# A transformer of two blocks on one core: squares of the norms between stages split over two engines, and next weights released at another point

## The chip, the cores and the metric

The kernel runs on 1 core of one Trainium2 chip, as one launch. The metric is the time of an execution in device microseconds (us); several executions are timed and their median is given. A profile is one further execution, recorded by the hardware profiler.

## The reference

x holds 256 tokens of 1024 fp32 channels. The first block has two layers of `proj = rms_norm(x) @ w_in`, attention beside a long convolution, and `x = x + rms_norm(m @ w_out)`. The second block has four stages, each of this form, with shift, scale and gate from a condition vector:

```python
h = rmsnorm(x, norm) * (1.0 + sc) + sh
y = stage(h)      # even_mixer, dense swiglu, s5_mixer, moe_swiglu
x = x + g * y
```

The norm is `x * rsqrt(mean(x * x) + eps)`: over the 1024 channels of each token the squares are summed, and every stage's first product needs it.

## The kernel before

**Tiles.** Tokens lie on the partitions, in two token tiles of 128 (`tt` 0 and 1), x is 128x1024 for each. Products are made in three parts: an fp32 operand is split (`split`, lines 205 to 211) into a high part, rounded by ScalarE (ACT, line 208), and a low part, the rest, by VectorE (DVE, line 211); `mm3` (lines 219 to 223) then adds high by high, low by high and high by low on TensorE (PE). Names end accordingly: `whi`, `wlo` for a chunk of weights (128x1024, made by `wchunk` from `raw`, which a DMA of SP's queue fills), `hTh`, `hTl` for the normed input with channels on the partitions.

**Between stages.** When the last stage has added its output to token tile `tt`, it calls `x_done(tt)`. This squares x and sums (`row_stats`: two halves of 512 channels, both on ACT, line 368), makes 1/sqrt on DVE in some eight instructions of 128x1 (`norm_stats`, lines 330 to 360), writes that factor on a diagonal `dg` (DVE, line 421), and `transposed` lets PE multiply x by it, 8 products of 128x128 in two groups of four (line 440; the trace shows two rows for each), which turns and scales x at once. DVE, or ACT for the first group, applies gain and shift (`hh`, lines 447 to 454) and `split` makes hTh and hTl of it. The places where this happens are called here: start (layer 0, 0 to 25 us), A (layer 0 to layer 1, at 285), B (to the mixer, at 560), C (to the dense FFN, at 722), D (to S5, at 932, kind "chunk") and E (to the experts, at 1060, kind "both", where z is made in place of dg and the router's product comes first); the others are of kind "plain". So 6 places by 2 tiles by 2 halves give 24 squares.

**Order.** The program is written stage by stage; a list scheduler then lays down for every engine one queue, which the engine runs in order. `issue_after(i)` keeps an instruction behind instruction i in it. In "plain" places the splits of the next two chunks of weights (HOLDP is 2) are held behind `self.hold`, the last ACT instruction so far, which there is the second square of tile 1; "chunk" holds none (HOLDC is 0), "both" holds four behind another point. PRIO, HH_BUFS (3 buffers for `hh`) and the rest of the numbers stay.

Of the kernel before, what the change touches and what calls it, by code (L numbers as in the profile page):

```python
# [14 lines left out]
AF = mybir.ActivationFunctionType  # L15
ALU = mybir.AluOpType
# [4 lines left out]
P = 128  # L21
# [97 lines left out]
class Net:  # L119
    def __init__(self, ctx, tc, a, out):  # L120
        self.ctx, self.tc, self.nc, self.a, self.out = ctx, tc, tc.nc, a, out
        self.uid, self.ring, self.extra, self.left, self.hold, self.held = 0, {}, 0, 0, None, 0
        self.tasks = []
        self.mq = tc.nc.gpsimd
        self.dq = (tc.nc.gpsimd, tc.nc.sync, tc.nc.scalar)[DQ]
        self.gate, self.pool_lo = [], 0
        self.rows, self.cols = {}, {}
        e = ctx.enter_context
        self.cst = e(tc.tile_pool(name="cst", bufs=1))
        self.act = e(tc.tile_pool(name="act", bufs=1))  # L130
        self.mod = e(tc.tile_pool(name="mod", bufs=1))
        self.sm = e(tc.tile_pool(name="sm", bufs=8))
        self.ps = e(tc.tile_pool(name="ps", bufs=1, space=PSUM))
        self.dram = e(tc.tile_pool(name="dr", bufs=1, space=DRAM))
        self.wp = e(tc.tile_pool(name="wp", bufs=1, reuse_waits="tile"))
        self.raws, self.hls = [(self.wp, RAW_BUFS)], [(self.wp, HL_BUFS)]
# [121 lines left out]
    def wchunk(self, src, k, n):  # L258

        out = []  # L260
        step = 1024 // n
        for k0 in range(0, k, step):
            kk = min(step, k - k0)
            raw = self.raw()[:, :kk * n]
            self.nc.sync.dma_start(raw.rearrange("p (k n) -> p k n", k=kk),
                                   src[k0 * P:(k0 + kk) * P].rearrange("(k p) n -> p k n", p=P))
            hi = self.turn(self.hls, "whi", F32R)[:, :kk * n]
            lo = self.turn(self.hls, "wlo", F32R)[:, :kk * n]
            self.pool_lo -= 1
            with self.tc.issue_after(self.hold) if self.held > 0 else nullcontext():  # L270
                self.split(hi, lo, raw, lo_eng="pool" if self.pool_lo >= 0 else "dve")
            self.held -= 1
            out += [(hi[:, i * n:(i + 1) * n], lo[:, i * n:(i + 1) * n]) for i in range(kk)]
        return out

# [86 lines left out]

    def row_stats(self, src):

        ss = []
        for n in range(2):
            ss.append(self.small())
            self.nc.scalar.activation(self.junk, src[:, n * 512:(n + 1) * 512], AF.Square, scale=1.0 / 32, accum_out=ss[n])
        return self.norm_stats(ss, 1e-6)

    def product(self, f, n=1):
# [24 lines left out]
    def x_done(self, tt):  # L396

        kind = self.nx[2]
        if self.hT is None:
            if kind == "both":  # L400
                self.hT = (self.t(self.act, [P, 8, S], "hTh"), None)
            else:
                self.hT = (self.t(self.act, [P, 8, S], "hTh", F32R), self.t(self.act, [P, 8, S], "hTl", F32R))
        x = self.x[:, tt, :]
        if kind == "both":
            rr = self.row_stats(x)
            after = self.latest(mybir.EngineType.Activation)
            self.z = [*(self.z if tt else ()), self.rows_z(tt, rr)]
            if tt == 1:
                with self.tc.issue_after(after) if T0_LAST else nullcontext():  # L410
                    self.transposed(0, self.z[0], None)
                self.transposed(1, self.z[1], None)
                self.hold, self.held = self.latest(mybir.EngineType.Activation), HOLD
                self.split_rows()
        else:

            rr = self.row_stats(x)
            if tt:
                self.hold, self.held = self.latest(mybir.EngineType.Activation), HOLDP if kind == "plain" else HOLDC
            dg = self.t(self.act, [P, P], "dg", bufs=2)  # L420
            self.nc.vector.tensor_scalar(dg, self.ident, *rr, ALU.mult, ALU.mult)
            self.transposed(tt, x, dg)
        self.set_gate("x")
        if tt == 1:
            self.pool_lo = POOL_LO
# [1519 lines left out]
HH_BUFS = 3  # L1945
# [126 lines left out]
HOLDP = 2  # L2072
HOLDC = 0
# [1 lines left out]
```

## Time and profile before

| | us |
|---|---|
| median of 3 runs | 1892.56 |
| range of the 3 runs | 1890.31 to 1893.56 |
| the profiled execution | 1882.28 |
| its span, first to last instruction | 1880.4 |
| PE busy | 1803.7 |
| DVE busy | 1517.6 |
| ACT busy | 1210.3 |

The profiled execution is one of its own and lies 10.3 us under the median; durations and waits are read from it. A busy time is the sum over an engine's instructions; the share of it over the whole span says little of a place where another engine sets the pace, so the places are read one by one. The mean granted clock of PE was 0.970 of full speed.

### The profile page before, as it was taken

How to read it: one execution, taken by the hardware profiler on the slowest of the kernel's cores; microseconds unless marked ns; L12 is line 12 of the kernel's file. 1: busy time of each engine (PE TensorE's matmuls, PEld its weight loads, DVE VectorE, ACT ScalarE, POOL GpSimd, SP SyncE). 2: the span in 40 equal slices, each digit the busy share in tenths (PEclk: the TensorE clock that was granted, in tenths of full speed). 3: DMA queues.
4: the chain of work that ended last, by engine and by line, in shares of the span. 5: the costliest groups of instructions: out<-in, count | busy, mean ns of one | idle time of the engine just before them, and what ended most of it. 6: DMA issues, size and time to landing. Idle time of an engine off the chain costs nothing.

```text
span 1880.4 us, 31046 instructions
## 1 busy us (share of the span) xinstructions
PE 1803.7 (96%) x11358; PEld 1536.1 (82%) x11358; DVE 1517.6 (81%) x2393; ACT 1210.3 (64%) x1670; POOL 195.9 (10%) x355
## 2 busy tenths in 40 slices
PE   7999998999999998999899899999999999999996
PEld 6887776988878768999799788888888888888875
DVE  6787667687558668975578789999999999999897
ACT  5664355564448526655454588887778787877775
POOL 0003232231330000111100100100001000100000
PEclk9999998999998969999998899999999999999998
DMA  7656785875775504988675779999999999999991
GB/s 258 202 155 214 247 287 199 282 250 199 255 248 166 167 12 144 291 258 256 218 264 215 272 266 378 340 355 343 377 344 349 348 380 355 346 373 356 344 355 44
DMA packets 268968, 503.45 MB, mean 268 GB/s; under 512 B 24690, under 2 KB 110516, under 8 KB 267272
## 3 DMA queue, kind: packets, MB, share of 16 engines
q1 hardware_dynamic: 247768, 445.84, 68.9%
q0 software_dynamic: 21040, 55.55, 8.4%
q8 instruction: 91, 1.49, 0.3%
q14 instruction: 69, 0.57, 0.1%
HBM read 485.35 MB, written 15.75 MB: 266 GB/s over the span
## 4 chain that ended last, share of the span: by engine, by line
PE 79%; issue 10%; DVE 5%; DMA 3%; ACT 2%; POOL 1%; POOLq 0%; ACTq 0%; DVEq 0%
PE A L221 12%; PE A L222 12%; PE A L223 12%; PE B L221 6%; PE B L222 6%; PE B L223 6%; PE A L323 4%; PE A L324 4%; PE A L325 4%; PE B L959 2%; DMA rawm<-in_e_mod_mix_w_dram 2%; DVE wlo L211 1%; PE B L440 1%; PE B L1756 1%; PE B L1101 1%
## 5 line engine op out<-in xcount | busy, mean ns | idle before, releaser
L211 DVE TENSOR_TENSOR wlo<-raw,whi 128x1024 fp32r<-128x1024 f32 x777 | 930.3, 1221 | 204.6 <-ACT whi L208 193.1
L208 ACT ACTIVATE whi<-raw 128x1024 fp32r<-128x1024 f32 x777 | 814.3, 1058 | 339.0 <-PE A L223 135.9
L221 PE MATMUL A<-whi,hTh 128*128 128x512 f32 (+1 forms) x752 | 285.6, 387 | 7.3 <-ACT hTh L208 4.8
L222 PE MATMUL A<-wlo,hTh 128*128 128x512 f32 (+1 forms) x752 | 289.2, 385 | 1.4 <-DVE wlo L211 1.2
L223 PE MATMUL A<-whi,hTl 128*128 128x512 f32 (+1 forms) x752 | 286.8, 383 | 0.9 <-DVE hTl L211 0.7
L323 PE MATMUL A<-hTh,whi 128*128 128x256 f32 x864 | 244.9, 284 | 3.8 <-ACT hTh L208 2.2
L324 PE MATMUL A<-hTl,whi 128*128 128x256 f32 x864 | 243.2, 282 | 0.8 <-DVE hTl L211 0.8
L325 PE MATMUL A<-hTh,wlo 128*128 128x256 f32 x864 | 243.7, 282 | 0.1
L221 PEld LDWEIGHTS A<-whi,hTh 128*128 128x128 f32 x752 | 142.3, 189 | 38.5 <-ACT hTh L208 5.9
L323 PEld LDWEIGHTS A<-hTh,whi 128*128 128x128 f32 x864 | 163.7, 190 | 7.9 <-issue 3.6
L222 PEld LDWEIGHTS A<-wlo,hTh 128*128 128x128 f32 x752 | 142.4, 189 | 33.8 <-DVE wlo L211 5.1
L223 PEld LDWEIGHTS A<-whi,hTl 128*128 128x128 f32 x752 | 142.3, 189 | 30.9 <-DVE hTl L211 2.1
L324 PEld LDWEIGHTS A<-hTl,whi 128*128 128x128 f32 x864 | 163.8, 190 | 2.7 <-DVE hTl L211 1.0
L325 PEld LDWEIGHTS A<-hTh,wlo 128*128 128x128 f32 x864 | 163.7, 190 | 2.0 <-issue 1.2
L222 PE MATMUL A<-wlo,xg 128*128 128x512 f32 (+1 forms) x384 | 143.2, 373 | 0.0
L223 PE MATMUL A<-whi,xg 128*128 128x512 f32 (+1 forms) x384 | 142.9, 372 | 0.0
L221 PE MATMUL A<-whi,xg 128*128 128x512 f32 (+1 forms) x384 | 141.6, 376 | 0.0
L222 PE MATMUL B<-wlo,mhh 128*128 128x512 f32 x352 | 138.6, 394 | 0.0
L223 PE MATMUL B<-whi,mhl 128*128 128x512 f32 x352 | 137.5, 391 | 0.0
L221 PE MATMUL B<-whi,mhh 128*128 128x512 f32 x352 | 120.8, 393 | 0.2 <-ACT mhh L208 0.2
L222 PEld LDWEIGHTS A<-wlo,xg 128*128 128x128 f32 x384 | 72.4, 189 | 12.9 <-DVE wlo L211 0.3
L223 PEld LDWEIGHTS A<-whi,xg 128*128 128x128 f32 x384 | 72.3, 188 | 12.5
(586 smaller groups left out, 2816.7 us busy)
## 6 DMA issues: line engine op xcount, KB each, us to landing
raw<-in_o_exp_up_dram SPq DMA_DIRECT2D x176, 512.0 KB, 5.7
raw<-in_o_exp_down_dram SPq DMA_DIRECT2D x176, 512.0 KB, 5.9
raw<-in_o_exp_gate_dram SPq DMA_DIRECT2D x174, 512.0 KB, 5.8
raw<-in_w_in_dram SPq DMA_DIRECT2D x96, 512.0 KB, 4.7
rawm<-in_e_mod_mix_w_dram POOLq DMA_DIRECT2D x24, 512.0 KB, 6.0
rawm<-in_e_mod_ffn_w_dram POOLq DMA_DIRECT2D x24, 512.0 KB, 6.1
rawm<-in_o_mod_mix_w_dram POOLq DMA_DIRECT2D x24, 512.0 KB, 5.6
rawm<-in_o_mod_ffn_w_dram POOLq DMA_DIRECT2D x24, 512.0 KB, 6.4
```

What stands on the lines that cost most here:

```text
L208: nc.scalar.activation(hi, src, AF.Copy)
L211: (nc.gpsimd if lo_eng == "pool" else nc.vector).tensor_tensor(lo, src, hi.bitcast(F32), ALU.subtract)
L221: nc.tensor.matmul(out, ah, bh, start=first, stop=False)
L222: nc.tensor.matmul(out, ah, bl, start=False, stop=False)
L223: nc.tensor.matmul(out, al, bh, start=False, stop=last)
L323: nc.tensor.matmul(o, wh[:, ms], xh[:, k, :], start=k == 0 and m == 0, stop=False, **kw)
L324: nc.tensor.matmul(o, wh[:, ms], xl[:, k, :], start=False, stop=False, **kw)
L325: nc.tensor.matmul(o, wl[:, ms], xh[:, k, :], start=False, stop=k == 7, **kw)
L440: nc.tensor.matmul(o, x[:, ks], dg, start=True, stop=True)
L959: nc.tensor.matmul(acc[32 * j:32 * j + 32, cs], silu[:, k:k + 1].broadcast_to([P, 32]), raws[i][:, k * P:(k + 1) * P], start=r == 0 and i ...
L1101: nc.tensor.matmul(pt[:, i, :], z[ps, ts], w[ps, ts], start=True, stop=True)
L1756: nc.tensor.transpose(ptr[:, i * P:(i + 1) * P], sg[:, i * P:(i + 1) * P], self.ident)
```

## The change

Of each norm's two squares the second is made on DVE, as one instruction that multiplies and sums (the trace shows it as a custom instruction and a read-out of 0.08 us; its product goes into a buffer of the ring `hh` and is not used). In `x_done` of kinds "plain" and "chunk" the hold is no longer the last square of tile 1 but `behind0`, the last ACT instruction of `transposed(0)`, which makes tile 0's hTh; and the first chunk after it (`spared`) isn't held. The `__init__` sets `spared` to 0.

```diff
@@ -267,9 +267,12 @@
             hi = self.turn(self.hls, "whi", F32R)[:, :kk * n]
             lo = self.turn(self.hls, "wlo", F32R)[:, :kk * n]
             self.pool_lo -= 1
-            with self.tc.issue_after(self.hold) if self.held > 0 else nullcontext():
+            with self.tc.issue_after(self.hold) if self.held > 0 and self.spared <= 0 else nullcontext():
                 self.split(hi, lo, raw, lo_eng="pool" if self.pool_lo >= 0 else "dve")
-            self.held -= 1
+            if self.spared > 0:
+                self.spared -= 1
+            else:
+                self.held -= 1
             out += [(hi[:, i * n:(i + 1) * n], lo[:, i * n:(i + 1) * n]) for i in range(kk)]
         return out
 
@@ -362,10 +365,10 @@
 
     def row_stats(self, src):
 
-        ss = []
-        for n in range(2):
-            ss.append(self.small())
-            self.nc.scalar.activation(self.junk, src[:, n * 512:(n + 1) * 512], AF.Square, scale=1.0 / 32, accum_out=ss[n])
+        ss = [self.small(), self.small()]
+        self.nc.scalar.activation(self.junk, src[:, :512], AF.Square, scale=1.0 / 32, accum_out=ss[0])
+        h = src[:, 512:]
+        self.nc.vector.tensor_tensor_reduce(self.t(self.act, [P, 4, P], "hh", bufs=HH_BUFS).rearrange("p k t -> p (k t)"), h, h, 1.0 / 1024, 0.0, ALU.mult, ALU.add, ss[1])
         return self.norm_stats(ss, 1e-6)
 
     def product(self, f, n=1):
@@ -416,10 +419,11 @@
 
             rr = self.row_stats(x)
             if tt:
-                self.hold, self.held = self.latest(mybir.EngineType.Activation), HOLDP if kind == "plain" else HOLDC
+                self.hold, self.held, self.spared = self.behind0, HOLDP if kind == "plain" else HOLDC, 1
             dg = self.t(self.act, [P, P], "dg", bufs=2)
             self.nc.vector.tensor_scalar(dg, self.ident, *rr, ALU.mult, ALU.mult)
             self.transposed(tt, x, dg)
+            self.behind0 = self.latest(mybir.EngineType.Activation)
         self.set_gate("x")
         if tt == 1:
             self.pool_lo = POOL_LO
```

Line numbers grow by 3 or 4 behind this (360 becomes 363, 421 becomes 424, 440 becomes 444, 447 becomes 451, 454 becomes 458); 208, 211 and 221 to 223 stay. Over the whole program DVE has 3039 rows in place of 3013, ACT 2151 in place of 2163 (12 squares and, in layer 0, 2 activation table loads fewer; some rows are grouped otherwise), PE 12408 for 12405 and SP 1422 for 1423 by grouping alone, POOL 224 as before.

DVE at the start. `sm` are the 128x1 values of a norm, `subln` is no part of it; `x_75` is x. Before, from the end of tile 0's norm to the first low part:

```order
L350 TENSOR_SCALAR sm_15_104<-sm_15_104 128x1
L421 TENSOR_SCALAR dg_110<-ident_78,sm_14_103,sm_15_104 128x128
L360 SCALAR_TENSOR_TENSOR sm_23_134<-sm_21_130,sm_22_132 128x1
L333 TENSOR_SCALAR sm_24_136<-sm_23_134 128x1
L342 SCALAR_TENSOR_TENSOR sm_25_138<-sm_24_136,sm_23_134 128x1
L347 SCALAR_TENSOR_TENSOR sm_26_139<-sm_25_138 128x1
L348 SCALAR_TENSOR_TENSOR sm_27_140<-sm_25_138 128x1
L349 SCALAR_TENSOR_TENSOR sm_26_139<-sm_26_139,sm_24_136 128x1
L350 TENSOR_SCALAR sm_27_140<-sm_27_140 128x1
L421 TENSOR_SCALAR dg_146<-ident_78,sm_26_139,sm_27_140 128x128
L447 TENSOR_TENSOR hh_117<-B_112,pre_83 128x512
L211 TENSOR_TENSOR wlo_172<-raw_169,whi_171 128x1024
```

Now, from tile 0's hh on (L371 is the square, its second row the read-out):

```order
L451 TENSOR_TENSOR hh_118<-B_113,pre_83 128x512
L211 TENSOR_TENSOR wlo_174<-raw_171,whi_173 128x1024
L451 TENSOR_TENSOR hh_127<-B_122,pre_83 128x512
L371 ISA hh_134,sm_23_132<-x_75 128x512
L371 ISA sm_23_132 128x1
L211 TENSOR_TENSOR hTl_93<-hh_118,hTh_92 128x4x128
L363 SCALAR_TENSOR_TENSOR sm_25_136<-sm_22_131,sm_23_132 128x1
L211 TENSOR_TENSOR hTl_93<-hh_127,hTh_92 128x4x128
L336 TENSOR_SCALAR sm_26_138<-sm_25_136 128x1
L211 TENSOR_TENSOR wlo_180<-raw_177,whi_179 128x1024
L345 SCALAR_TENSOR_TENSOR sm_27_140<-sm_26_138,sm_25_136 128x1
L211 TENSOR_TENSOR wlo_186<-raw_183,whi_185 128x1024
```

Tile 1's norm stood ahead of every low part, its dg (`dg_146`) ahead of tile 0's hh. It now stands behind the first, with two more inside; its dg follows five rows further down.

PE at the start, `A` being the products of tile 0 (A_167, now A_169) and tile 1 (A_168, now A_170). Before:

```order
L440 MATMUL B_112<-dg_110,x_75 128x128 x4
L440 MATMUL B_121<-dg_110,x_75 128x128 x4
L440 MATMUL B_148<-dg_146,x_75 128x128 x4
L440 MATMUL B_157<-dg_146,x_75 128x128 x4
L221 MATMUL A_167<-whi_171,hTh_92 128x512
L222 MATMUL A_167<-wlo_172,hTh_92 128x512
L223 MATMUL A_167<-whi_171,hTl_93 128x512
```

Now, the end of tile 0's 18 products and what follows:

```order
L221 MATMUL A_169<-whi_185,hTh_92 128x512
L222 MATMUL A_169<-wlo_186,hTh_92 128x512
L223 MATMUL A_169<-whi_185,hTl_93 128x512
L444 MATMUL B_150<-dg_148,x_75 128x128 x4
L444 MATMUL B_159<-dg_148,x_75 128x128 x4
L552 MATMUL B_255<-ffeat_247,fw_52_249 64x256
L221 MATMUL A_170<-whi_173,hTh_92 128x512
L222 MATMUL A_170<-wlo_174,hTh_92 128x512
L223 MATMUL A_170<-whi_173,hTl_93 128x512
```

Tile 1's eight transposes have moved from behind tile 0's to behind all 18 products of tile 0 with the first three chunks. At A, B and C they stand in the same way behind 18, 24 and 48.

DVE at D, `dg` being the diagonals of the two tiles and B the results of PE's transposes. Before:

```order
L421 TENSOR_SCALAR dg_10482<-ident_78,sm_2030_10475,sm_2031_10476 128x128
L360 SCALAR_TENSOR_TENSOR sm_2041_10518<-sm_2039_10514,sm_2040_10516 128x1
L333 TENSOR_SCALAR sm_2042_10520<-sm_2041_10518 128x1
L342 SCALAR_TENSOR_TENSOR sm_2043_10522<-sm_2042_10520,sm_2041_10518 128x1
L347 SCALAR_TENSOR_TENSOR sm_2044_10523<-sm_2043_10522 128x1
L348 SCALAR_TENSOR_TENSOR sm_2045_10524<-sm_2043_10522 128x1
L349 SCALAR_TENSOR_TENSOR sm_2044_10523<-sm_2044_10523,sm_2042_10520 128x1
L350 TENSOR_SCALAR sm_2045_10524<-sm_2045_10524 128x1
L421 TENSOR_SCALAR dg_10530<-ident_78,sm_2044_10523,sm_2045_10524 128x128
L454 TENSOR_SCALAR hh_10501<-B_10496,colo_mod_mix_3923 128x128 x4
L211 TENSOR_TENSOR hTl_10465<-hh_10489,hTh_10464 128x4x32x4
L454 TENSOR_SCALAR hh_10549<-B_10544,colo_mod_mix_3923 128x128 x4
```

Now:

```order
L424 TENSOR_SCALAR dg_10491<-ident_78,sm_2039_10484,sm_2040_10485 128x128
L458 TENSOR_SCALAR hh_10510<-B_10505,colo_mod_mix_3927 128x128 x4
L371 ISA hh_10526,sm_2049_10524<-x_75 128x512
L371 ISA sm_2049_10524 128x1
L211 TENSOR_TENSOR hTl_10473<-hh_10498,hTh_10472 128x4x32x4
L363 SCALAR_TENSOR_TENSOR sm_2051_10528<-sm_2048_10523,sm_2049_10524 128x1
L211 TENSOR_TENSOR hTl_10473<-hh_10510,hTh_10472 128x4x32x4
L336 TENSOR_SCALAR sm_2052_10530<-sm_2051_10528 128x1
L345 SCALAR_TENSOR_TENSOR sm_2053_10532<-sm_2052_10530,sm_2051_10528 128x1
L350 SCALAR_TENSOR_TENSOR sm_2054_10533<-sm_2053_10532 128x1
L351 SCALAR_TENSOR_TENSOR sm_2055_10534<-sm_2053_10532 128x1
L352 SCALAR_TENSOR_TENSOR sm_2054_10533<-sm_2054_10533,sm_2052_10530 128x1
```

The two dg stood eight rows apart with nothing but the norm between; now hh of tile 0 (4 parts), the square of tile 1 and two hTl stand between, and tile 1's dg follows two rows further down.

## Rows read from the trace of the kernel before

**Rows 1.** The page: busy time of each engine, and the chain that ended last by engine

```profile
PE 1803.7 (96%) x11358; PEld 1536.1 (82%) x11358; DVE 1517.6 (81%) x2393; ACT 1210.3 (64%) x1670; POOL 195.9 (10%) x355
PE 79%; issue 10%; DVE 5%; DMA 3%; ACT 2%; POOL 1%; POOLq 0%; ACTq 0%; DVEq 0%
```

**Rows 2.** Busy us by stretch (start, A to D, one stage): PE, PEld, DVE, ACT, POOL, PEclk

```profile
8.00:22.20 14.20, 12.47 (x53) 9.85 (x54) 9.46 (x20) 7.02 (x12) 0.00 (x0) 1.00 0.88 304
284.60:302.00 17.40, 9.79 (x84) 8.54 (x84) 13.87 (x39) 8.09 (x16) 1.51 (x3) 0.71 0.39 125
558.80:576.00 17.20, 11.10 (x49) 8.86 (x49) 14.91 (x61) 10.20 (x24) 6.60 (x9) 0.70 0.43 125
721.60:734.00 12.40, 7.36 (x42) 7.17 (x41) 11.25 (x25) 9.40 (x20) 0.91 (x4) 0.72 0.55 174
930.20:946.30 16.10, 7.42 (x36) 6.89 (x35) 12.66 (x34) 9.68 (x18) 0.78 (x5) 0.77 0.98 362
302.00:400.00 98.00, 98.00 (x929) 86.23 (x928) 68.30 (x113) 58.69 (x93) 28.46 (x56) 1.00 0.81 269
```

**Rows 3.** Groups by line and form, ACT, line 368: count, busy us, mean ns, idle before

```profile
L368 ACT ACTIVATE junk<-x 128x512 f32<-128x512 f32 x24 | 15.1, 629 | 33.4 <-DVE x L1015 17.4 <-DVE x L900 10.2 <-DMA x<-in_x_dram 5.7
```

**Rows 4.** Groups by line and form, DVE: multiplies with a sum; last, a two-source fp32 one

```profile
L740 DVE CUSTOM_DVE_ANT_0 k<-B,nbias 128x256 f32<-128x256 f32 x32 | 12.3, 414 | 2.4 <-PE B L735 2.4
L1059 DVE CUSTOM_DVE_ANT_0 fx_s<-B,fmask 128x128 f32<-128x128 f32 x8 | 2.3, 290 | 2.9 <-PE B L1053 2.9
L740 DVE DVE_READ_ACCUMULATOR2_ANT sm<- 128x1 f32 x32 | 2.6, 82 | 0.0
L900 DVE SCALAR_TENSOR_TENSOR x<-k,sm,x 128x512 f32<-128x512 f32 x8 | 5.7, 749 | 0.1
```

**Rows 5.** The page's costliest groups: the low and the high parts of the weights

```profile
L211 DVE TENSOR_TENSOR wlo<-raw,whi 128x1024 fp32r<-128x1024 f32 x777 | 930.3, 1221 | 204.6 <-ACT whi L208 193.1
L208 ACT ACTIVATE whi<-raw 128x1024 fp32r<-128x1024 f32 x777 | 814.3, 1058 | 339.0 <-PE A L223 135.9
```

**Rows 6.** Timeline of the start, DVE twice, then PE: start us, duration us, instruction

```profile
11.72 0.34 DVE L421 TENSOR_SCALAR dg<-ident,sm,sm 128x128 f32<-128x128 f32 x1
14.66 1.23 DVE L211 TENSOR_TENSOR wlo<-raw,whi 128x1024 fp32r<-128x1024 f32 x1 [2.00 <-ACT whi L208]
...
26.21 0.86 PE L221 MATMUL A<-whi,hTh 128*128 128x512 f32 x3
```

**Rows 7.** Timeline of A, PE

```profile
289.32 3.75 PE L440 MATMUL B<-dg,x 128*128 128x128 f32 x16 [4.67 <-DVE sm L342]
295.72 0.50 PE L221 MATMUL A<-whi,hTh 128*128 128x512 f32 x1 [2.64 <-ACT hTh L208]
```

**Rows 8.** Timeline of B, PE

```profile
574.13 1.95 PE L440 MATMUL B<-dg,x 128*128 128x128 f32 x16
```

**Rows 9.** Timeline of C, ACT, then PE

```profile
728.45 1.15 ACT L208 ACTIVATE hTh<-hh 128x512 fp32r<-128x512 f32 x2
...
728.56 3.78 PE L440 MATMUL B<-dg,x 128*128 128x128 f32 x16 [5.04 <-DVE dg L421]
```

**Rows 10.** Timeline of D, DVE, then PE

```profile
936.92 0.35 DVE L421 TENSOR_SCALAR dg<-ident,sm,sm 128x128 f32<-128x128 f32 x1
939.86 1.37 DVE L454 TENSOR_SCALAR hh<-B,colo_mod_mix 128x128 f32<-128x128 f32 x4 [2.59 <-PE B L440]
941.14 1.04 DVE L211 TENSOR_TENSOR hTl<-hh,hTh 128x512 fp32r<-128x512 f32 x1
...
936.07 6.72 PE L440 MATMUL B<-dg,x 128*128 128x128 f32 x32 [5.71 <-DVE sm L360]
944.98 0.50 PE L323 MATMUL A<-hTh,whi 128*128 128x256 f32 x2 [2.19 <-ACT hTh L208]
```

**Rows 11.** Timeline of E, DVE, then PE

```profile
1068.53 0.55 DVE L466 TENSOR_SCALAR xg<-x,sm,sm 128x512 f32<-128x512 f32 x1
...
1070.25 1.95 PE L438 MATMUL B<-ident,xg 128*128 128x128 f32 x8
```

More of the change, by code (lines that the diff above doesn't have):

```diff
@@ L121, in __init__ @@
         self.ctx, self.tc, self.nc, self.a, self.out = ctx, tc, tc.nc, a, out
-        self.uid, self.ring, self.extra, self.left, self.hold, self.held = 0, {}, 0, 0, None, 0
+        self.uid, self.ring, self.extra, self.left, self.hold, self.held, self.spared = 0, {}, 0, 0, None, 0, 0
         self.tasks = []
```

## The prediction

> **What bounds the kernel now.** I read first the busy times and the chain: TensorE (PE) is busy 1803.7 of 1880.4 us, 96%, and holds 79% of the chain that ended last [rows 1]. Time can therefore come only from the 4% in which PE stands still, and anything that makes PE wait longer goes straight to the end. Second, the windows: between two stages PE is busy only 9.79 of 17.4 us (A, layer 0 to layer 1), 11.10 of 17.2 (B, to the mixer), 7.36 of 12.4 (C, to the dense FFN), 7.42 of 16.1 (D, to S5), its granted clock falls to 0.70-0.77 there (it reads 1.00 in the stages), and VectorE (DVE) is the fuller of its helpers, 13.87 us against 8.09 of ScalarE (ACT) in A; in a stage, as in the last row, PE is busy 98.00 of 98.00 [rows 2]. So each of six places counts by itself: the start, A to D, and E (to the experts). At each I walked the two queues' orders with the durations of the rows and asked when PE gets tile 1's last operand.
>
> **The squares.** Removed: 12 ACT squares of 0.629 us and their read-outs [rows 3]. Added: 12 DVE squares with sum. The trace has none at 128x512 with both sources in SBUF; the same form, one source in PSUM, costs 0.290 at 128 columns and 0.414 at 256, with 0.082 to read out, and a two-source fp32 pass over 512 columns of SBUF (line 900) takes 0.75 [rows 4]. By 0.12 per 128 columns, 512 take about 0.66, 0.74 with the read-out; the ends are 0.5 (256 columns plus nothing much) and 0.9 (twice the 256). Two halves that ran one behind the other on ACT (about 0.75 each) now run side by side, so alone a norm is ready up to 0.7 us earlier; but DVE is in order, and what stands ahead of the square there decides. [...]
>
> **The held weights.** Of the next stage's chunks (high part 1.058 on ACT, low part 1.221 on DVE [rows 5]), one is no longer held, and two wait for tile 0's input instead of tile 1's square. Nothing is added on ACT; what moves is where low parts stand on DVE, and with that PE's order: tile 1's 16 transposes stood right behind (or two matmuls behind) tile 0's and now stand behind all of tile 0's matmuls (18, 18, 24, 48 at the start, A, B, C). SP's weight loads keep their order but for neighbours, and POOL's 224 rows none moved.
>
> **Start, +3.2.** Tile 1's dg is ready at 11.72 now, long before the first low part, which starts at 14.66 when the weight has come; PE reaches the fourth chunk at 26.21 [rows 6]. After: tile 1's square stands behind that low part and its norm between two more. From 14.66: three low parts (3.6), four passes of about 0.65 (hh, square, two hTl), a norm chain of about 1.1 give dg at 22.0. PE ends tile 0's 18 matmuls at about 22.4, transposes until 25.2, has tile 1's hTl at 25.7 and ends its 18 at 0.23 each at 29.4, against 26.21. Ends: +2.0 (transposes at their shortest, 1.95 [rows 8]) and +3.5.
>
> **A, -0.8.** PE waits 4.67 for dg of tile 0, then 2.64 for hTh behind three high parts on ACT [rows 7]. After: the free chunk's low part stands ahead of tile 0's x update (1.1 later), the DVE square gives 0.2 back: PE starts at 290.3 instead of 289.3. hTh no longer waits behind high parts: tile 0's matmuls start at about 294 instead of 295.72, wait some 1.3 for the second low part, and tile 1's follow about 0.8 earlier than now. Ends -2.0 and +1.0, by whether those matmuls run at the clock of 0.71 or of 1.00.
>
> **B, +2.0.** The same low part ahead of tile 0's x makes PE start 0.7 later. Tile 1's transposes now begin at 574.13 with tile 0's other matmuls behind them [rows 8]; after, they come last, at about 576, and PE has nothing while hh, hTh and hTl of tile 1 (1.36 and twice 0.65) are made: 2.1 us. Less 0.8 for a tile 0 that starts without the high parts ahead of it. Ends +0.5 and +3.0.
>
> **C, -0.7.** PE waits 5.04 for tile 1's dg, and tile 0's hTh comes only at 728.45, behind four high parts [rows 9]. After: tile 0's 48 start at about 726, but their chunks come at the pace of DVE's low parts, and tile 1's hh to hTl chain (about 2.2) is bare at the end. Of 5 us most is given back. Ends -2.2 and +1.0.
>
> **D, +4.7.** No chunk is held here, before or after. What moves is the square: tile 1's stood on ACT, which was free, and its dg was there at 936.92, so that PE ran all 32 transposes in 6.72 without a gap from 936.07 and the first matmul at 944.98 [rows 10]. After, DVE has tile 0's hh (four parts, 1.37) ahead of tile 1's square and both hTl (1.04 each) between square and dg. That hh waits for tile 0's second half, half of the 6.72 behind 935.8: 939.5. Then 1.3 + 0.7 + 2.1 + 0.9 (norm) gives dg at 944.5; 3.4 of transposes; first matmul at 949.7. Ends +2.5 (both hTl find their place beside waits) and +5.2.
>
> **E, +0.5.** No chunk moves. ACT is freed of the square ahead of tile 0's hTh (1.7 earlier), but DVE has tile 0's hTh ahead of tile 1's square, and the router's rows in its norm: tile 1's xg at about 1070.4 instead of 1068.53, beside PE's start of its transposes at 1070.25 [rows 11]. Ends -1.0 and +2.0.
>
> Two activation table loads fewer in layer 0 lie on an ACT that is busy 64% [rows 1]: nothing, and what else the scheduler shuffles I take as 0, within 2 us. **Sum:** 3.2 - 0.8 + 2.0 - 0.7 + 4.7 + 0.5 = +8.9. The profiled execution took 1882.28 (its span of 1880.4 and 1.88 around it), 10.3 under the median of 1892.56; I put the difference on the median: 1901.5. All lower ends together give about 0, all upper ones +16.
>
> **Rivals.** Faster: the chunks before tile 1's transposes do what an overlap would do. At A, B and C PE waits 2.64, about 3.2 (two waits) and 5.04 between tile 0's and tile 1's work; if tile 0's matmuls fill these and tile 1's hTl is ready at their end, 10.9 are won; if the start loses 2 and D 2.5, 6.4 remain: 1886. It decides by whether DVE's low parts and tile 1's hh, hTh, hTl end before tile 0's matmuls do. For it: the idle of rows 7 and 9. Against it: PE's order has nothing behind tile 1's transposes, and DVE is the fuller engine in each window.
> No change: losses are there, but a later wait that was there anyway swallows them (the low lists of A and C come true and D costs half): between -3.8 and +3.8, which is 0.2% and about what a measurement of this kernel can tell: 1889 to 1896. Against it: 98.00 of 98.00 in the stage leaves nothing to swallow with.
> [...]
> That the change does nothing is out: DVE's and PE's queues are in another order.
>
> **How the numbers follow.** Forecast with the sum's ends 0.56, slow square 0.05: slower by over 0.2% 0.61. No change 0.22. Faster 0.17. The range takes the no-change case, most of the bounds and half of the faster case: 1886 to 1909; the forecast's own range is 1897 to 1909.
>
> **What would show it.** Start: the first matmul of the fourth chunk at about 29.4. A and C: a shorter idle ahead of tile 0's matmuls, with DVE's low parts as releaser in place of ACT's hTh. B: idle of about 2 ahead of tile 1's matmuls. D: PE's 32 transposes in two groups with about 5.5 idle between, released by dg, and the first projection at about 949.7 less the shift. L371 at about 0.66. I am wrong if D's group stays whole, if PE reaches the fourth chunk before 27, or if tile 1's matmuls at A to C follow its transposes at once.

## The result, and the profile after

| | before | after |
|---|---|---|
| median of 4 runs, us | 1891.43 | 1911.86 |
| their range, us | 1880.83 to 1893.56 | 1908.46 to 1912.21 |
| the profiled execution, us | 1882.28 | 1912.21 |
| its span, us | 1880.4 | 1910.3 |
| mean granted clock of PE | 0.970 | 0.961 |

The change makes the kernel slower: the ratio is 1.0111, interval 1.008 to 1.0142, or +20.4 us on the medians. The forecast of +8.9 had the sign, not the size.

On the page of the kernel after, PE is busy 18.4 us more than in [rows 1] for the same 11358 products, and DVE and DMA hold more of the chain:

```profile
PE 1822.1 (95%) x11358; PEld 1546.4 (81%) x11358; DVE 1525.0 (80%) x2417; ACT 1200.8 (63%) x1644; POOL 194.6 (10%) x355
...
PE 75%; issue 10%; DVE 7%; DMA 6%; ACT 2%; POOL 0%; SPq 0%; POOLq 0%; ACTq 0%; DVEq 0%
```

More busy time for the same products means that more of them ran at a lower pace, at a mean granted clock of 0.961 in place of 0.970; it is no new work. Of the 29.9 us by which the span grew, 18.4 are such busy time and only 11.5 are time in which PE stood idle.

**The square** (DVE, line 371, all twelve; duration in ns as shortest, median, longest, then first and last start):

```profile
L371 DVE CUSTOM_DVE_ANT_0 hh<-x x12: 679/682/799, 4.2 to 1095.6; 128x512 f32<-128x512 f32 x12
L371 DVE DVE_READ_ACCUMULATOR2_ANT sm<- x12: 76/82/83, 4.8 to 1096.3; 128x1 f32 x12
```

0.68, where 0.66 had been estimated, and 0.08 to read out. From the 0.414 at 256 columns and one source in PSUM [rows 4] that is 0.13 for each 128 columns more, with both fp32 sources in SBUF, against the 0.12 of the estimate. A square much slower than estimated, to which the forecast gave 0.05 as the slow square, is out.

**The start.** DVE, timeline (start, duration, instruction, idle before it and what ended it):

```profile
14.18 1.23 DVE L211 TENSOR_TENSOR wlo<-raw,whi 128x1024 fp32r<-128x1024 f32 x1 [2.55 <-ACT whi L208]
15.32 0.68 DVE L451 TENSOR_TENSOR hh<-B,pre 128x512 f32<-128x512 f32 x1
15.93 0.68 DVE L371 CUSTOM_DVE_ANT_0 hh<-x 128x512 f32<-128x512 f32 x1
...
17.21 0.68 DVE L211 TENSOR_TENSOR hTl<-hh,hTh 128x512 fp32r<-128x512 f32 x1
...
20.72 0.34 DVE L424 TENSOR_SCALAR dg<-ident,sm,sm 128x128 f32<-128x128 f32 x1
```

PE, same stretch:

```profile
14.72 0.80 PE L221 MATMUL A<-whi,hTh 128*128 128x512 f32 x1 [3.37 <-ACT hTh L208]
...
17.86 0.63 PE L221 MATMUL A<-whi,hTh 128*128 128x512 f32 x1
...
23.79 1.95 PE L444 MATMUL B<-dg,x 128*128 128x128 f32 x16
...
30.95 0.86 PE L221 MATMUL A<-whi,hTh 128*128 128x512 f32 x3
```

The square of tile 1 waits behind a low part that itself waits for its weight, and behind tile 0's second hh. Its input was there long before: in e5 below, where nothing of tile 0 stands ahead of it, it starts at 10.30, when its half of x has landed. Tile 1's dg is there at 20.72 in place of 11.72, and PE reaches the fourth chunk at 30.95 in place of 26.21 [rows 6].

**D.** DVE, then PE:

```profile
960.13 0.35 DVE L424 TENSOR_SCALAR dg<-ident,sm,sm 128x128 f32<-128x128 f32 x1
964.42 1.36 DVE L458 TENSOR_SCALAR hh<-B,colo_mod_mix 128x128 f32<-128x128 f32 x4 [3.94 <-PE B L444]
965.70 0.68 DVE L371 CUSTOM_DVE_ANT_0 hh<-x 128x512 f32<-128x512 f32 x1
966.31 1.13 DVE L211 TENSOR_TENSOR hTl<-hh,hTh 128x512 fp32r<-128x512 f32 x1
967.35 1.02 DVE L211 TENSOR_TENSOR hTl<-hh,hTh 128x512 fp32r<-128x512 f32 x1
969.17 0.34 DVE L424 TENSOR_SCALAR dg<-ident,sm,sm 128x128 f32<-128x128 f32 x1
```

```profile
960.63 3.75 PE L444 MATMUL B<-dg,x 128*128 128x128 f32 x16 [5.39 <-DVE dg L424]
969.57 3.78 PE L444 MATMUL B<-dg,x 128*128 128x128 f32 x16 [5.19 <-DVE dg L424]
974.36 0.79 PE L326 MATMUL A<-hTh,whi 128*128 128x256 f32 x2 [1.01 <-ACT hTh L208]
```

One group of 32 transposes [rows 10] has become two of 16 with 5.19 of idle between, and DVE itself stood idle 3.94 ahead of tile 0's hh: the square was ready to run and stood behind an instruction that wasn't.

**B.** PE, and two windows (columns as in [rows 2], the last but two the clock):

```profile
581.82 0.80 PE L221 MATMUL A<-whi,hTh 128*128 128x512 f32 x1 [0.58 <-ACT hTh L208]
...
592.00 1.95 PE L444 MATMUL B<-dg,x 128*128 128x128 f32 x16
...
595.31 0.50 PE L221 MATMUL A<-whi,hTh 128*128 128x512 f32 x1 [1.36 <-ACT hTh L208]
...
596.49 0.68 PE L223 MATMUL A<-whi,hTl 128*128 128x512 f32 x1 [0.45 <-DVE hTl L211]
```

```profile
581.80:590.00 8.20, 7.31 (x16) 4.90 (x17) 8.20 (x32) 3.47 (x4) 1.39 (x4) 0.51 0.36 80
...
592.00:600.00 8.00, 6.19 (x28) 4.79 (x27) 6.33 (x34) 5.49 (x12) 0.00 (x0) 0.79 0.15 48
```

Tile 0's products run at a granted clock of 0.51 from 581.8 to 590, and behind the bare chain of tile 1 the clock falls once more, to 0.52 from 596.5 to 600. The same 153 products, from 554 to 590 in before and then after:

```profile
554.00:590.00 36.00, 29.90 (x155) 24.79 (x154) 30.72 (x121) 21.91 (x43) 8.60 (x13) 0.86 0.55 160
```

```profile
567.00:609.20 42.20, 35.11 (x156) 28.12 (x155) 35.24 (x161) 21.03 (x39) 8.57 (x13) 0.77 0.43 129
```

PE was busy 5.2 us longer and idle only 1.0 longer (6.1, then 7.1): most of the loss at B is pace, not waiting.

**A.** PE, tile 1's transposes and its first product:

```profile
314.46 1.28 PE L444 MATMUL B<-dg,x 128*128 128x128 f32 x10
315.67 1.52 PE L963 MATMUL B<-rawm,silu 128*32 128x128 f32 x48
317.11 0.94 PE L444 MATMUL B<-dg,x 128*128 128x128 f32 x6
317.80 0.48 PE L221 MATMUL A<-whi,hTh 128*128 128x512 f32 x1
```

Tile 1's products follow its transposes at once here, since 48 other products (line 963) stand among the transposes.

**Where the 29.9 us between the two profiled executions lie.** For this table, and for the experiments, each PE row that stands in both timelines in the same order is matched, and its start before is taken from its start now. The figure tells how far a run is behind the profile of before at that point; what it grows by between two points was lost there.

| behind the profile of before, us | start done | before A | A done | before B | B done | scan of the mixer done | C done | D done | end |
|---|---|---|---|---|---|---|---|---|---|
| (its time, us) | 26 | 280 | 400 | 551 | 586 | 705 | 900 | 989 | 1850 |
| after | 4.7 | 13.8 | 11.9 | 12.7 | 19.2 | 26.4 | 24.9 | 28.1 | 29.9 |

Lost: 4.7 at the start, 9.0 in layer 0 behind it (6.0 of them by 145 us), 0.8 in layer 1, 6.5 at B, 7.2 in the mixer, 3.2 at D, 1.8 at E. Won: 1.9 at A, 1.5 at C. Of the 29.9, 9.1 are the profile of before being that much under its median of 1891.43, and 0.4 the profile of after being over its own: 20.4 are left.

### The profile page after: what moved, and what is told of

It is laid out like the page before. It is cut to its first block, busy times and chain, and to the rows that moved or that the text cites. A ratio compares the mean times of both kernels' runs of the same rounds, so it can differ in the third digit from the quotient of the medians.

```text
span 1910.3 us, 31037 instructions
## 1 busy us (share of the span) xinstructions
PE 1822.1 (95%) x11358; PEld 1546.4 (81%) x11358; DVE 1525.0 (80%) x2417; ACT 1200.8 (63%) x1644; POOL 194.6 (10%) x355
## 4 chain that ended last, share of the span: by engine, by line
PE 75%; issue 10%; DVE 7%; DMA 6%; ACT 2%; POOL 0%; SPq 0%; POOLq 0%; ACTq 0%; DVEq 0%
PE A L223 12%; PE A L222 12%; PE A L221 12%; PE B L221 6%; PE B L222 6%; PE B L223 6%; PE A L326 4%; PE A L327 4%; PE A L328 4%; PE B L963 2%; DVE wlo L211 2%; DMA rawm<-in_e_mod_mix_w_dram 2%; PE B L1105 1%; PE B L444 1%; DMA raw<-in_o_exp_gate_dram 1%
## 5 line engine op out<-in xcount | busy, mean ns | idle before, releaser
L222 PE MATMUL A<-wlo,hTh 128*128 128x512 f32 (+1 forms) x752 | 293.2, 390 | 1.8 <-DVE wlo L211 1.6
L223 PE MATMUL A<-whi,hTl 128*128 128x512 f32 (+1 forms) x752 | 290.8, 388 | 3.7 <-DVE hTl L211 3.4
L223 PEld LDWEIGHTS A<-whi,hTl 128*128 128x128 f32 x752 | 144.4, 192 | 36.4 <-DVE hTl L211 7.3
```

The costliest lines, as they stand in the source:

```text
L222: nc.tensor.matmul(out, ah, bl, start=False, stop=False)
L223: nc.tensor.matmul(out, al, bh, start=False, stop=last)
```

## The experiments

Two theories at first. The **queue** theory: the square's product goes into the ring `hh`, whose three buffers go out in the program's order, so that tile 1's square can't stand ahead of tile 0's second hh; what costs is the square's place in DVE's queue. Its rivals: the **holds** (weights released earlier fill DVE and push PE's order about), and the **work** itself (12 times 0.76 on the fuller engine). For all experiments a counter `site` of the norms (0 the start, 1 to 4 A to D, 5 E) and two tuples switch the parts:

```diff
+        if self.site not in SQ:
+            self.nc.scalar.activation(self.junk, h, AF.Square, scale=1.0 / 32, accum_out=ss[1])
+            return self.norm_stats(ss, 1e-6)
...
-                self.hold, self.held, self.spared = self.behind0, HOLDP if kind == "plain" else HOLDC, 1
+                self.held = HOLDP if kind == "plain" else HOLDC
+                self.hold, self.spared = (self.behind0, 1) if self.site in HB else (self.latest(mybir.EngineType.Activation), 0)
...
+SQ = (0, 1, 2, 3, 4, 5)
+HB = (0, 1, 2, 3, 4, 5)
```

In the three batches the kernel before had medians of 1893.25 (16 runs), 1892.88 (31) and 1894.18 (21). All of them, with the matched starts as above:

| run | SQ / HB | ratio (interval) | us against before | start done | before A | A done | before B | B done | scan done | C done | D done | end |
|---|---|---|---|---|---|---|---|---|---|---|---|---|
| e1 | all / none | 1.012 (1.0094 to 1.0146) | +24.7 | 4.3 | 14.6 | 19.0 | 19.3 | 24.9 | 31.7 | 33.1 | 36.4 | 38.6 |
| e2 | none / all | 1.0023 (1.0008 to 1.0039) | +2.3 | -0.9 | ~2.5 | 9.6 | 9.6 | 9.3 | 16.4 | 12.6 | 10.6 | 11.5 |
| e3 | 0 / 0 | 1.0078 (1.0051 to 1.0104) | +15.1 | 4.0 | 14.9 | 25.0 | 24.9 | 28.6 | 28.7 | 28.5 | 28.4 | 29.0 |
| e4 | 1-5 / 1-5 | 1.0022 (1.0006 to 1.0037) | +4.8 | -0.1 | 0.3 | 0.4 | 0.8 | 5.6 | 12.2 | 9.6 | 13.0 | 13.2 |
| e5 | all / all, own buffer | 1.0006 (0.9991 to 1.0022) | +1.6 | -0.5 | 11.2 | 10.9 | 11.4 | 9.1 | 17.5 | 14.5 | 13.0 | 14.8 |
| e6 | all / none, own buffer | 1.0027 (1.0015 to 1.0038) | +6.2 | 0.2 | 2.8 | 6.0 | 5.9 | 7.9 | 15.4 | 16.9 | 16.4 | 20.0 |
| e7 | 4 / none | 1.0026 (1.0008 to 1.0043) | +6.2 | 0.1 | 4.3 | 5.5 | 5.8 | 5.7 | 11.4 | 11.6 | 16.2 | 18.7 |
| e8 | all, tile 0 only / none | 0.9997 (0.9985 to 1.0009) | -0.5 | -0.2 | 1.8 | 3.2 | 3.0 | 3.1 | 3.1 | 3.0 | 0.5 | 2.4 |
| e9 | all / 1-4, own buffer | 0.9972 (0.996 to 0.9984) | -5.1 | 0.3 | 4.5 | 4.1 | 4.2 | 4.1 | 11.2 | 8.2 | 7.9 | 8.2 |
| e10 | 0 / none | 1.008 (1.0057 to 1.0103) | +14.8 | 5.3 | 16.0 | 19.0 | 19.4 | 21.6 | 27.5 | 27.3 | 27.0 | 27.5 |
| e11 | none / 0 | 1.0058 (1.0039 to 1.0076) | +11.5 | -0.9 | 6.9 | 19.4 | 19.8 | 23.1 | 23.1 | 23.2 | 21.5 | 23.2 |

(For e7, D is read at 945 us, behind its transposes; e2's figure before A is read at 230.) The profile of before is shorter than its usual execution, so a run of about its time mostly ends some 8 to 15 behind it (e8, itself profiled in a short one, 2.4); the timed difference is the verdict, and the columns tell the place. Each column comes from one execution: e7, whose rows on PE stand in before's order throughout, still shifts by 4.2 in layer 0 and by 1.2 at A, so differences of that size in one column prove nothing.

**e1, squares alone; e2, holds alone.**

```diff
-HB = (0, 1, 2, 3, 4, 5)
+HB = ()
```

> Only the squares are as in the change (12 on VectorE); the holds are as in the kernel before. Theory S (the squares' place in VectorE's queue costs the time, at the start, at B and at D): nearly the whole loss stays, 15 to 20 us slower than before; the fourth chunk's first matmul on PE comes 4 to 5 us late and D's transposes fall into two groups with some 5 us between. Theory H (the loss comes from the chunks that are released at another point): within 5 us of the kernel before.

```diff
-SQ = (0, 1, 2, 3, 4, 5)
+SQ = ()
```

> Only the holds are as in the change; all 24 squares are on ScalarE. Theory S: within 4 us of the kernel before or some us faster, D's 32 transposes in one group, the start as before. Theory H: 10 us slower or more.

The squares alone cost 24.7, as much as the whole change (the intervals of the two overlap); the holds alone 2.3. In e1 the start costs 4.3 and D about 4.5, as with the change, and A costs 4.4 where the change wins 1.9. So the loss comes with the squares. That the holds give some of it back isn't clear of noise here; e9 against e6 shows it below.

**e3, the change at the start alone; e4, everywhere else.**

```diff
-SQ = (0, 1, 2, 3, 4, 5)
-HB = (0, 1, 2, 3, 4, 5)
+SQ = (0,)
+HB = (0,)
```

> The whole change at the start alone; the other five places as before, but the scheduler lays the rest of layer 0 in another order behind it. In the trace of the change PE stood 4.5 us back at the fourth chunk and 10.7 us back at the end of layer 0's filters (before's 145 us). Theory S with the start's own loss only: 4 to 5 us slower. Theory O (the start's shift also makes the scheduler lay layer 0 in a worse order): 10 to 13 us slower, with PE already 10 us back by before's 145 us.

```diff
-SQ = (0, 1, 2, 3, 4, 5)
-HB = (0, 1, 2, 3, 4, 5)
+SQ = (1, 2, 3, 4, 5)
+HB = (1, 2, 3, 4, 5)
```

> The change everywhere but at the start. Layer 0's queue on PE is then as before. Theory O: 8 to 10 us slower than before (20 less the start's 11), lost at B and D. Theory S with the start's own loss only: 15 us slower. If the clock in the scan of the mixer (0.50 for longer in the change's trace) belongs to the change's order at B, this run shows it too, 7 us of it; if it comes and goes by itself, it may not.

15.1 and 4.8 make 19.9, the 20.4 of the change; e3 lost more than either theory said, e4 less than either. Three quarters of the loss hang on the first place, though the start itself is only 4.0 late: e3 is 10.0 behind by 145 us and 14.9 before A, then loses 10 more around A, where its code is that of before. In e4, B costs 4.8 and D 4.5; C wins 2.6.

**e10 and e11 split the start:** square alone (`SQ = (0,)`, `HB = ()`) and hold alone (`SQ = ()`, `HB = (0,)`).

> Only the square at the start, into the hh ring; the start's hold and all else as before. Theory W: tile 1's transposes behind tile 0's 18 matmuls as in e3, the fourth chunk 4 to 5 us late, and with the layer's other order 12 to 18 us slower in all: the square makes e3's whole loss. If the hold had a part in it: under 8.

> Only the hold at the start as in the change; all squares on ScalarE. The start itself is as before to 1 us (fourth chunk); the order of the rest of layer 0 differs from before's and from the change's. Theory P: layer 0 loses some us behind the start, 2 to 8 in all. If the order of layer 0 doesn't matter by itself: within 2 us of before.

Either alone costs nearly the whole: 14.8 and 11.5. e11 is the telling one, for its start isn't late at all (-0.9). Its square is where it was; with the hold changed at one place the list scheduler laid all of layer 0 and what follows in another order, and in its trace that order loses 7.8 up to A and 12.6 around it. So what the start costs is for the larger part not its own delay but the order of the stages behind it. e10 lost what had been expected, e11 more. One piece of such an order could be seen in the trace of after: where DVE is full, PE waits for its split (windows of after, DVE's column 6.00 of 6.00, then PE):

```profile
122.00:128.00 6.00, 3.13 (x24) 2.61 (x22) 6.00 (x10) 3.44 (x5) 0.00 (x0) 1.00 0.60 178
```

```profile
125.10 0.51 PE L221 MATMUL B<-kf,fwdh 128*128 128x512 f32 x1 [0.47 <-ACT kf L208]
128.55 0.50 PE L222 MATMUL B<-kf,fwdh 128*128 128x512 f32 x1 [2.94 <-DVE kf L211]
```

In before DVE was as full there (10.00 of 10.00 from 115 us), and as many rows (seven) stood on it from the first of line 605, there 601, to that split; but PE had 22 products of a projection (lines 323 to 325) between the two products of kf, and so hardly waited:

```profile
117.35 0.39 PE L221 MATMUL B<-kf,fwdh 128*128 128x512 f32 x1
...
120.65 0.51 PE L222 MATMUL B<-kf,fwdh 128*128 128x512 f32 x1 [0.34 <-DVE kf L211]
```

The same wait is 2.95 in e1, e3 and e10, and 0.34 in e9, whose start is before's. Behind it the clock of after reads 0.50 from 129.10 to 135.80 us; in before it reads 1.00 from 26 to 280 us. Around A another wait is common to e3 and e11, here e11's ACT, then PE:

```profile
358.79 0.63 ACT L584 ACTIVATE k<-k 128x512 f32<-128x512 f32 x1 [4.86 <-DMA k<-in_flt_deltas_dram]
```

```profile
362.24 0.58 PE L326 MATMUL A<-hTh,whi 128*128 128x256 f32 x1 [3.43 <-ACT whi L208]
```

ACT, in order, waits for a row of layer 1's filter, and PE for the high part that stands behind it (3.88 and 3.42 in e3; in before ACT waits 0.92 there and PE not at all). Both runs lose 5.4 us in these few microseconds. Why that row landed so late is open: in e3 and e11 one weight load more than in before stands ahead of its own, but so it does in e9 and e10, which don't lose there.

**e7, the square at D alone:** `SQ = (4,)`, `HB = ()`.

> Only the square at D on VectorE, into the hh ring as in the change; all else as before, so that the queues up to 918 us are those of before. Theory W: PE's transposes at D in two groups and 4 to 5 us lost there, of which 1 comes back later; 3 to 5 us slower. Theory V with its loss spread over the places: 2 us or less.

Up to D its queues are those of before. Between 900 and 945 us it goes from 11.6 to 16.2 behind: D costs 4.5, as the working had it (4.7). It shows something else: with before's own order it is 11.6 behind the profile of before ahead of D. So that profile was a short execution; 5.7 of the 11.6 lie in the mixer's scan (5.7 to 11.4, below).

**e5 and e6, a buffer of its own.** The product nobody reads goes into a scratch tile; it and ACT's `junk` are bf16, to save room (the sums stay fp32).

```diff
-        self.nc.vector.tensor_tensor_reduce(self.t(self.act, [P, 4, P], "hh", bufs=HH_BUFS).rearrange("p k t -> p (k t)"), h, h, 1.0 / 1024, 0.0, ALU.mult, ALU.add, ss[1])
+        self.nc.vector.tensor_tensor_reduce(self.junk2, h, h, 1.0 / 1024, 0.0, ALU.mult, ALU.add, ss[1])
...
-        self.junk = self.t(self.act, [P, 512], "junk")
+        self.junk = self.t(self.act, [P, 512], "junk", mybir.dt.bfloat16)
+        self.junk2 = self.t(self.act, [P, 512], "junk2", mybir.dt.bfloat16)
```

e5 is the whole change so, e6 the squares alone (`HB = ()`).

> The whole change, but the square on VectorE writes its unused product into a buffer of its own (two scratch tiles in bf16 in place of one in fp32, since the memory has no room for a second fp32 one; the sums stay fp32) instead of one of the ring of three that hh uses. Theory W (the ring ties tile 1's square behind tile 0's second hh in VectorE's queue, and that costs the time at the start and at D): tile 1's dg is early at the start, D's transposes stand in one group, the fourth chunk's first matmul comes within 1 us of before's, and the total is within 5 us of before. Theory V (the squares' work on VectorE, the fuller engine, costs the time): still 12 us slower or more.

> The squares alone (holds as before), with their own buffer as in the run e5. Theory W: of the 23 us that the squares alone cost at least 15 are gone, and D's transposes stand in one group. Theory V: 20 us slower again.

The same squares, in the same number and on the same engine: 20.4 becomes 1.6 and 24.7 becomes 6.2. D in e5, DVE, then PE:

```profile
949.60 0.68 DVE L374 CUSTOM_DVE_ANT_0 junk<-x 128x512 bf16<-128x512 f32 x1
950.20 0.35 DVE L429 TENSOR_SCALAR dg<-ident,sm,sm 128x128 f32<-128x128 f32 x1
951.55 0.35 DVE L429 TENSOR_SCALAR dg<-ident,sm,sm 128x128 f32<-128x128 f32 x1
954.18 1.37 DVE L463 TENSOR_SCALAR hh<-B,colo_mod_mix 128x128 f32<-128x128 f32 x4 [2.28 <-PE B L449]
```

```profile
950.69 5.23 PE L449 MATMUL B<-dg,x 128*128 128x128 f32 x32 [5.88 <-DVE sm L363]
959.22 0.50 PE L326 MATMUL A<-hTh,whi 128*128 128x256 f32 x2 [3.29 <-ACT hTh L208]
```

The square stands ahead of tile 0's hh again, the second dg follows the first by 1.35, and PE has its 32 transposes in one group. The square takes 0.69 (median, into bf16; 0.68 into fp32 in after) and ACT's 0.63 as before, so the types cost at most 0.01 us here; what has changed is the square's place, and with it the order that the scheduler lays. e6 shows the same at D between 900 and 945 us: 16.9 to 16.9, where e1 went from 33.1 to 37.6. The queue theory holds for 18.8 of the 20.4, and the work theory can't be the cause of these; whether work or order makes the 6.2 that e6 keeps is open.

**e8, DVE squares for tile 0 only** (still into `hh`):

```diff
-        if self.site not in SQ:
+        if self.site not in SQ or tt not in (0,):
```

> VectorE squares for token tile 0 alone, at all six places, into the hh ring; tile 1's on ScalarE, holds as before. Nothing of the ring stands ahead of tile 0's square. Theory W: within 3 us of before, PE's order at all six places as before. Theory V: half of the squares' loss, 10 us or more. The scan of the mixer (GLA) is as before in the queues: if its stretch at the clock of 0.50 is longer than in the profile of before here too, the 7 us there are not the change's.

0.9997: half of the squares on DVE through the ring, and no loss. They have no hh of another tile ahead of them.

**e9, the best of both:** own buffer, all squares on DVE, the new hold at A to D, the old one at the start (`HB = (1, 2, 3, 4)`).

> As e5 (squares on VectorE with their own buffer, chunks released behind tile 0's input), but at the start the hold is that of the kernel before. PE's order in layer 0 is then that of before. Theory P (what was left of e5's gain between the stages was lost again in layer 0, by the order that the start's hold made the scheduler choose): layer 0 ends 8 us earlier than in e5, A, B and C keep their gain; 3 to 7 us faster than before. Without P: as e5, within 2 us of before.

1889.06 (1883.08 to 1891.83, 12 runs) against 1894.18: faster than before by 0.28%, interval 0.16% to 0.4%. Its start, PE, keeps one group:

```profile
10.86 5.91 PE L449 MATMUL B<-dg,x 128*128 128x128 f32 x32 [10.86 <-DVE dg L429]
...
26.51 0.86 PE L221 MATMUL A<-whi,hTh 128*128 128x512 f32 x3
```

It is 0.3 behind the profile of before at the start and 1.9 by 145 us, where e5, which differs by the hold at the start alone, is 7.2 behind. At C it wins 3.1 (11.2 to 8.2), as e2 (3.8), e5 (3.1) and e4 (2.6) do, while e1 and e6, without the new holds, lose 1.5 there: that is the holds' gain. Between e6 and e9 only the holds at A to D differ, and e9 is 11.3 faster against its kernel before. Not tried: a scratch in fp32, or a ring of more than three buffers.

## Why the prediction was right and wrong

| term | forecast | measured (after) | elsewhere |
|---|---|---|---|
| start | +3.2 | +4.7 | e3 +4.0, e10 +5.3 |
| A | -0.8 | -1.9 | |
| B | +2.0 | +6.5 | e4 +4.8 |
| C | -0.7 | -1.5 | e4 -2.6 |
| D | +4.7 | +3.2 (+4.7 at 945) | e7 +4.5 |
| E | +0.5 | +1.8 | e4 +0.2 |
| the rest | 0, within 2 | layer 0 +9.0 | e3 +10.9 |

**Right:** the sign; the square at 0.66 (0.68; the slow square, in the forecast with 0.05, no run shows: the twelve took 0.68 to 0.80); the mechanism at D, to some tenths and by the rows foretold (two groups, 5.19 of idle released by dg); that tile 1's square stands behind tile 0's hh on DVE, at the start and at D; the signs of the start, B, C and D (A's -1.9 and E's +1.8 have the forecast's sign too, but e7 shifts as far there with before's order on PE, 1.2 and 2.5); and putting the difference on the median, not on the short profiled execution.

**The step that failed** is "what else the scheduler shuffles I take as 0, within 2 us". The six places come to +12.8 in the trace; layer 0 behind the start adds 9.0 (some 3 of which, between 145 and 280 us, are within what runs with before's queues also show: e4 0.6, e7 4.4). From 26 to 280 us of before and 30.9 to 294 of after, PE's idle grows from 8.0 to 12.3, and the same 1899 products take 250.8 in place of 246.0. e11 settles it: no delay at the start, 11.5 lost. The traces show where the order costs in two spots (PE's 2.94 for kf, and 3.4 behind the filter's row in e3 and e11); the rest of it was not followed to its waits.

**A premise that failed:** "Time can therefore come only from the 4% in which PE stands still". 18.4 of the 29.9 us between the two profiles are busy time of PE for the same products. The sum priced waits and hardly the lower clock beside them; it weighed the clock at A alone.

**Mis-sized: B.** The idle forecast there was 2.1 and measured 1.36 + 0.45, and over the whole place PE's idle grew by 1.0. What the sum left out is the clock: tile 0's products followed one another at 0.43 us until 589.90, against 0.23 behind it, at a granted clock of 0.51, and tile 1's again from 596.98 to 599.96. In before the stretch held 0.70 over 17.2 us [rows 2] and was at 1.00 behind it, from 576 to 586; tile 1's transposes stood there behind 13 of tile 0's products, not two. **The start** is off in the same way: products there stood 0.43 apart from 17.86 to 22.98, while the sum took 0.23. B shows the same 0.43 at a clock of 0.51, and by that pace the clock here is put at the same, an estimate. The profile's 1.00 for that stretch is no reading: its first record of the clock is at 23.21 us, where the pace changes. In e1, whose products ran at the same 0.43, the records begin earlier and read 0.50:

```profile
15.20:21.90 6.70, 5.53 (x13) 3.81 (x13) 6.07 (x16) 2.15 (x3) 0.00 (x0) 0.50 0.64 207
```

**A and C.** At A tile 0's products came as foretold, without a wait for hTh and with one of 0.76 for DVE's low part. But tile 1's followed its transposes at once, one of the prediction's own signs of being wrong: it had read that PE's order has nothing behind tile 1's transposes, and 48 products among them covered the chain. That is the faster rival's case, at one place of three. At C the idle of 5.04 shrank to 1.36 and 0.81 ahead of tile 0's products and 1.14 and 0.23 ahead of tile 1's; ACT's hTh and DVE's hTl released them, not a low part.

**The mixer's scan** took part in the trace difference and is not the change's doing. Between 653 and 663 us of before PE runs the same rows behind the same wait; timeline and windows of before:

```profile
653.02 0.30 PE L1066 MATMUL B<-ident,fx_s 128*128 128x128 f32 x1 [1.76 <-DVE sm L1062]
```

```profile
655.00:660.00 5.00, 4.31 (x27) 3.04 (x26) 3.99 (x10) 1.99 (x5) 0.00 (x0) 1.00 0.00 2
660.00:665.00 5.00, 4.36 (x22) 3.30 (x21) 2.77 (x9) 2.15 (x4) 0.00 (x0) 1.00 0.01 3
```

and of after:

```profile
672.24 0.45 PE L1070 MATMUL B<-ident,fx_s 128*128 128x128 f32 x1 [1.76 <-DVE sm L1066]
```

```profile
674.00:680.00 6.00, 6.00 (x34) 5.01 (x31) 3.21 (x6) 0.49 (x1) 0.00 (x0) 0.50 0.00 0
680.00:686.00 6.00, 5.31 (x14) 3.41 (x13) 3.11 (x12) 2.10 (x6) 0.00 (x0) 0.50 0.01 3
```

The clock read 1.00 there in one execution and 0.50 in the other. e1, e2, e4, e5, e6, e7, e9 and e10 lose 5.7 to 8.4 in the scan too, e7 among them with before's order on PE; e3, e8 and e11 lose nothing.

## What to carry to other kernels

An output that nobody reads still has a place in a ring, and here the ring put a 0.68 us instruction behind another tile's work: with it the change cost 20.4 us, with a tile of its own 1.6. So give scratch its own tile. Before moving work to an in-order engine, read what would stand ahead of it there and what that waits for; the engine's load says little (at D DVE stood idle for 3.94 us while the square waited). Where a list scheduler lays the order, a shift early on re-lays whole stages: price that from a run of that place alone, not at nothing. And price the clock beside the waits of PE: at B 1.0 us more of idle came with 5.2 us more of busy time for the same products, at a granted clock of 0.77 in place of 0.86.

## What the runs showed of the hardware

The multiply-and-sum over 128x512 with both fp32 sources in SBUF took 0.68 us on DVE, as long as line 211's difference of two SBUF tiles over 512 columns at the start (0.68), with 0.08 for the sum; ACT's square took 0.63 [rows 3]. The same rows of the mixer's scan behind the same wait of 1.76 ran at a granted clock of 1.00 in one execution and 0.50 in another, about 7 us apart, and the profile of before was 9 us off its kernel's median: compare traces by place, and times by medians. From 17.86 to 22.98 us of after, ahead of the trace's first clock record, a window reads 1.00 though products followed one another at 0.43, as at B at a clock of 0.51: there, go by the distance between products.
